# Backward steps of a bidirectional recurrence: queues in program order, z's loads ahead of late stores, and output rows split by VectorE where they are made

## The chip, the core and the metric

The kernel runs on one core of a Trainium2 chip. It uses all engines of that core: TensorE (PE) for matmuls, VectorE (DVE), ScalarE (ACT) and GpSimd (POOL) for the rest, and SyncE (SP), whose queue issues every DMA of the part that matters here. The metric is the device time of one execution in microseconds (us); less is better.

## The reference

The model has two layers over 2048 latent tokens and 256 context tokens of width 1024. The change lies in layer 1, which is cut here to what it computes:

```python
def odd_mixer(h, hc, w_in, conv_w, conv_b, w_a, b_a, w_i, b_i, lam, w_out, need_ctx):
    xr, g = _split(h @ w_in, (C_WIDTH, C_WIDTH))
    z = depthwise_conv(xr, conv_w, conv_b)             # and z_c from the context
    for d, reverse in ((0, False), (1, True)):
        a_c, b_c = rglru_coeffs(z_c, w_a[d], b_a[d], w_i[d], b_i[d], lam[d])
        s_c = linear_scan(a_c, b_c, 0, reverse)
        h0 = s_c[:, 0] if reverse else s_c[:, -1]
        a_l, b_l = rglru_coeffs(z, w_a[d], b_a[d], w_i[d], b_i[d], lam[d])
        s_l = linear_scan(a_l, b_l, h0, reverse)
        h_lat = s_l if h_lat is None else h_lat + s_l
    return (h_lat * silu(g)) @ w_out

def rglru_coeffs(z, w_a, b_a, w_i, b_i, lam):          # z @ w in 4 diagonal blocks of 256
    r, ig = sigmoid(z @ w_a + b_a), sigmoid(z @ w_i + b_i)
    log_a = -LRU_C * r * softplus(-lam)
    return exp(log_a), sqrt(-expm1(2 * log_a)) * (ig * z)

x = x + gate * odd_mixer(...)                          # then a final RMSNorm
```

All of it is fp32.

## The kernel before

The 18 tiles of 128 tokens are worked as 9 pairs of 256 tokens (`L = NPAIR = 9`; pair 0 is the context). An fp32 product is made of three matmuls: each operand is split into a rounded high part and the rest (`split`: a copy on ACT or a CAST on DVE or POOL, then a subtract), and `mm3` multiplies high by high, low by high and high by low. Channels lie on the partitions, 8 tiles of 128, which are worked as four blocks `b` of 256 channels (tiles of 128x512: two channel tiles by 256 tokens).

Layer 1 is one pipeline of steps `s` = 0 to 24, in a loop that writes the program order out by hand. Each step has a projection, a gate part, or both:

- projection: `xr` (the first half of `w_in`, `xr_mm`) of pair `s` in steps 0 to 8; `g` (`g_mm`) in steps 9 to 16; the output (`out_mm`) in steps 17 to 24. Each is four groups of matmuls into PSUM, `px` 0 to 3.
- gates: forward for pair `s - 3` in steps 3 to 11, backward in steps 12 to 20, in the pairs' order 0, 8, 7, 6, 5, 4, 3, 2, 1. A step's gate part is, for each `b`, `gates_mm` (the matmuls `pr` and `pig` with the split tile `zhl`), `gates_act` (two sigmoids on ACT that read `r` and `ig`, and POOL's multiply of `ig` by `z`); then `coeff` and `root` (tanh, exp and square root on ACT, three operations on DVE for each `b`), and `scan` for blocks 0 and 1, and for 2 and 3. In the backward direction the scan's result is added to the forward one (`hf`) and multiplied by the gate projection (`gs`), both read back from DRAM.
- `zsplit` splits `z` of the next step's pair into `zhl`, its block 2 behind the fourth gate matmuls of the step. The order of a step on ACT is: sigmoids of the four blocks, `zhl` of blocks 0 to 3 in between, then the coefficients.

What is carried between steps lies in DRAM: `zs` (z by pair), `hfs` (forward results), `gs_`, `y1s` (the products that the output projection reads), `x1s`. PE, ACT and DVE run in the order of this program from step 1 on (`tc.manual_schedule`); SP's queue and POOL are ordered by the scheduler. The four `wo` tiles (2 MB each, in two halves of 1 MB) are loaded from `kept` copies by `hook`s: `wo`[0] and [1] in step 16, `wo`[2] and [3] in step 17. In step 17 `px` 0 and 1 use the first two, `px` 2 and 3 the last two. For the output `op_load` brings `y1s` back as `opr`, and `op_split` splits it, in steps 17 to 20 by ACT copies and POOL subtracts, later with DVE subtracts.

The `post` of a projection's group 3 is deferred into the next step (`tails`): in the steps with `g` the `gs` of `px` 3 is made and stored behind the sigmoids of block 0 in program order of the next step, and on DVE behind the scans of the step before.

Of the kernel before, what the change touches and what calls it, by code (L numbers as in the profile page):

```python
# [33 lines left out]
U_AT = 5  # L34
T_PE = 14
MOD_AT = 8
WO1_AT = (2, 4, 6, 8, 10, 11, 12, 13)
# [3 lines left out]
def backbone_kernel(ctx: ExitStack, tc: tile.TileContext, a, out):  # L41
# [968 lines left out]
    L = NPAIR  # L1010
    order = [0] + list(range(L - 1, 0, -1))

    with ExitStack() as c4:
# [13 lines left out]
        def halves_load(s):  # L1027

            for q in range(4):
# [16 lines left out]
        def op_split(s, k):  # L1046
            raw = opr.pop((s, k))
            tag = "zhl" if s > 2 * L + 2 and (s - 2 * L - 3) % 2 == 0 else "h1p"
            for q in range(2):
                t = b1.tile([P, 2, 2, U], F32R, tag=tag, name="op", bufs=4)  # L1050
                split(t[:, 0], t[:, 1], raw[:, 2 * q:2 * q + 2], eng_lo=dve if s > 2 * L + 2 else pool)
                for c in range(2):
# [76 lines left out]
        def scan(d, i, bs_):  # L1129
# [3 lines left out]
            for b in bs_:  # L1133
# [7 lines left out]
                e = 0 if d else U - 1  # L1141
                e_c = dve if d and i == order[L - 5] else pool
                e_c.tensor_copy(carry[d][:, 2 * b:2 * b + 2].unsqueeze(2), T[:, :, e:e + 1])  # L1143
            for k in range(2 if i and d else 0):
                for b in bs_:
# [4 lines left out]
                    else:  # L1150
                        dve.scalar_tensor_tensor(T, T, 0.5, hg, ALU.mult, ALU.mult)
            for b in bs_:
                T = ris.pop((d, i, b))[2]
                if i:
                    sp.dma_start((y1s if d else hfs)[i][:, 2 * b:2 * b + 2], T)

# [42 lines left out]
        def g_mm(s, i, b):  # L1199
# [10 lines left out]
            return mm, post  # L1210

        def out_mm(s, i, b):
            x, half = divmod(b, 2) if s > 2 * L - 1 else (b % 2, b // 2)
# [7 lines left out]
            def post():  # L1221
                if half == 0:
                    xts[t] = []
                    for h in range(2):
                        xt = b1.tile([P, 512], F32, tag="gs", name="xt", bufs=4)
                        sp.dma_start(xt, x1s[t][:, 512 * h:512 * h + 512])
                        xts[t].append(xt)
                    xts[t].append(b1.tile([P, 2], F32, tag="ss", name="ss", bufs=2))
                xt, ss, po = xts[t][half], xts[t][2], pxs.pop(b)
                dve.tensor_tensor(xt, xt, po, ALU.add)  # L1230
                act.activation(po, xt, AF.Square, accum_out=ss[:, half:half + 1])  # L1231
                if late:
                    late.pop()()
                end = s == 3 * L - 3 and x == 1
                if half == 0:
# [5 lines left out]
                if end:  # L1241
                    og = b1.tile([P, 512], F32, tag="G", name="og", bufs=1)
                    dve.tensor_tensor(og, xt, FG[:, 512:], ALU.mult)
# [62 lines left out]

        def z_load(s):
            nx = gate(s + 1)
            if nx and nx[0]:
                for b in range(4):  # L1310
                    sp.dma_start(z_tile(*nx, b), zs[nx[1]][:, 2 * b:2 * b + 2])

        def step(s):
# [21 lines left out]

            z_load(s)
            if s + 1 < 2 * L - 1:
                halves_load(s + 1)
            first = early(s) and s != 2 * L - 1
            if first:  # L1340
                op_split(s, 0)
            G(gmm, 0)
            G(gates_act, 0)
            tail(3)
            if early(s) and not first:
                op_split(s, 0)
# [37 lines left out]
            hook("s0")  # L1384
            if source(s + 1) and s + 1 >= 2 * L - 1:
                for k in range(2):
                    op_load(s + 1, k)
                    if not early(s + 1):
                        op_split(s + 1, k)
            if E:  # L1390
                post(0)
            G(scan, (0, 1))
            mm(3)
            if not E:
                post(2)
            elif s > 2 * L + 1:
                post(1)
            G(scan, (2, 3))
            n = gate(s + 1)
            if n and n[0] and n[1]:  # L1400
                for b in range(4):
                    load_hg(n[1], b)
# [4 lines left out]
        def early(s):  # L1407

            return 2 * L - 1 <= s <= 2 * L + 2

        tails = []
# [56 lines left out]
```

## Time and profile before

| | us |
|---|---|
| median of 3 runs (1996.14 to 1998.95) | 1996.38 |
| the profiled execution's own time | 1996.66 |
| its span | 1994.9 |
| PE busy in the span | 1897.1 (95%) |
| DVE busy | 1468.3 (74%) |
| ACT busy | 1095.8 (55%) |
| POOL busy | 599.7 (30%) |

The profiled execution's time is 1.76 us more than its span, and 0.28 us above the median. Times in the trace are us from the span's start; L1207 is line 1207 of the kernel. A step is taken to start at its first gate matmul: step 13 at 1583.50, 14 at 1619.48, 15 at 1654.04, 16 at 1689.46, 17 at 1731.82, 18 at 1765.12, 19 at 1811.68, 20 at 1854.90. The number in brackets at the end of a row of a timeline is the time for which the engine was idle before it, and what ended that. The clock in a stretch is what PE was granted, 1.00 being full speed.

### The profile page before, as it was taken

Reading aid. Unit: us, or ns where it says so; the run is one execution under the profiler, and the core shown is the slowest. Engines: PE = TensorE matmul, PEld = TensorE weight load, DVE = VectorE, ACT = ScalarE, POOL = GpSimd, SP = SyncE. Lnnn points to the kernel's source line nnn. Section 1 sums busy time; section 2 is a strip of 40 time slices with the busy share of each in tenths; the row PEclk is TensorE's granted clock in tenths of the full one; section 3 lists DMA queues with packets and bytes.
Section 4 is the critical chain, followed back from the end, with each engine's and each line's share of the span. In section 5 each row is a group of like instructions: output and inputs, shape, how many; then the busy total and the mean of one; then the engine's idle time right before and its main releaser. Section 6 shows DMA issues by size and latency. Waiting matters only on the chain.

```text
span 1994.9 us, 33922 instructions
## 1 busy us (share of the span) xinstructions
PE 1897.1 (95%) x12223; PEld 1699.0 (85%) x12223; DVE 1468.3 (74%) x3103; ACT 1095.8 (55%) x2221; POOL 599.7 (30%) x793
## 2 busy tenths in 40 slices
PE   7889999999999899989999999999999999878998
PEld 3778888988888688778888899999999999867777
DVE  7788989787755687636777663998986666877863
ACT  6656656666645343414545552767667666656621
POOL 2745656454423211200000000434421121334310
PEclk8999999999999899989999999999999999989999
DMA  9355444361344798365656574233565554965442
GB/s 348 125 183 188 160 156 150 134 212 56 122 156 160 251 331 314 122 242 218 247 191 242 200 263 149 75 135 120 207 231 212 183 193 154 323 209 185 133 165 88
DMA packets 184788, 375.80 MB, mean 188 GB/s; under 512 B 18694, under 2 KB 78858, under 8 KB 176428
## 3 DMA queue, kind: packets, MB, share of 16 engines
q1 hardware_dynamic: 184620, 373.64, 53.5%
q8 instruction: 96, 1.57, 0.3%
q14 instruction: 72, 0.59, 0.1%
HBM read 246.41 MB, written 127.17 MB: 187 GB/s over the span
## 4 chain that ended last, share of the span: by engine, by line
PE 70%; DVE 11%; ACT 6%; DMA 5%; issue 5%; POOL 1%; SPq 1%; POOLq 0%; DVEq 0%; ACTq 0%
PE px L89 6%; PE px L90 6%; PE px L91 6%; PE pu L89 4%; PE pu L90 4%; PE pu L91 4%; PE po L90 3%; PE po L89 3%; PE po L91 3%; PE po L572 3%; PE ptp L560 2%; DVE macc L230 2%; PE pg L89 2%; DMA zf<-zs 2%; PE pg L90 2%
## 5 line engine op out<-in xcount | busy, mean ns | idle before, releaser
L89 PE MATMUL px<-op,w 128*128 128x256 f32 x1088 | 308.1, 283 | 0.0
L90 PE MATMUL px<-op,w 128*128 128x256 f32 x1088 | 307.9, 283 | 0.0
L91 PE MATMUL px<-op,w 128*128 128x256 f32 x1088 | 307.9, 283 | 0.0
L90 PEld LDWEIGHTS px<-op,w 128*128 128x128 f32 x1088 | 208.9, 192 | 0.0
L89 PEld LDWEIGHTS px<-op,w 128*128 128x128 f32 x1088 | 208.9, 192 | 0.0
L91 PEld LDWEIGHTS px<-op,w 128*128 128x128 f32 x1088 | 208.9, 192 | 0.0
L542 POOL TENSOR_SCALAR s<-s,ri 128x640 f32<-128x640 f32 (+2 forms) x144 | 133.5, 939 | 97.9 <-DVE ri L539 93.8
L83 ACT ACTIVATE pT<-ptp 128x512 fp32r<-128x512 f32 (+1 forms) x192 | 99.6, 535 | 92.7 <-PE ptp L560 89.5
L534 ACT ACTIVATE s<-s,mn 128x641 f32<-128x641 f32 (+2 forms) x144 | 113.3, 788 | 64.2 <-DVE mn L516 58.6
L1099 POOL TENSOR_TENSOR ig<-ig,zf 128x512 f32<-128x512 f32 x72 | 109.7, 1532 | 97.7 <-ACT ig L1097 89.8
L86 DVE TENSOR_TENSOR zhl<-zf,zhl 128x512 fp32r<-128x512 f32 x72 | 59.8, 838 | 103.4 <-ACT zhl L83 103.1
L572 PE MATMUL po<-pT,v 128*128 128x256 f32 x656 | 130.1, 296 | 6.1 <-DVE pT L86 4.5
L86 DVE TENSOR_TENSOR pT<-ptp,pT 128x512 fp32r<-128x512 f32 (+1 forms) x192 | 114.3, 604 | 23.6 <-ACT pT L83 22.8
L900 DVE STREAM_TRANSPOSE h1T<-hrow 32x256 f32<-32x256 f32 x224 | 97.7, 436 | 31.1 <-ACT hrow L952 28.1
L89 PE MATMUL px<-w,op 128*128 128x512 f32 x256 | 102.9, 402 | 15.8 <-ACT px L1231 15.8
L162 POOL TENSOR_SCALAR ms<-ss 128x1 f32<-128x1 f32 x36 | 10.0, 278 | 350.2 <-ACT junk L160 343.2
L572 PEld LDWEIGHTS po<-pT,v 128*128 128x128 f32 x656 | 98.6, 189 | 17.3 <-DVE pT L86 9.2
L560 PE MATMUL ptp<-ident,s 128*128 128x128 f32 x656 | 103.6, 273 | 3.4 <-POOL s L542 1.9
L1143 POOL COPY carry<-T 128x2 f32<-128x2 f32 x68 | 35.0, 514 | 232.1 <-DVE T L1140 225.7
L90 PE MATMUL px<-w,op 128*128 128x512 f32 x256 | 102.2, 399 | 0.0
L91 PE MATMUL px<-w,op 128*128 128x512 f32 x256 | 101.9, 398 | 0.0
L89 PE MATMUL pr<-zhl,w 128*128 128x256 f32 x288 | 83.4, 289 | 16.7 <-ACT r L1097 16.7
(277 smaller groups left out, 6186.1 us busy)
## 6 DMA issues: line engine op xcount, KB each, us to landing
hp<-h0s SPq DMA_DIRECT2D x45, 1024.0 KB
op<-h1s SPq DMA_DIRECT2D x64, 512.0 KB
mraw<-in_w_mod SPq DMA_DIRECT2D x48, 512.0 KB
h0s<-hT SPq DMA_DIRECT2D x18, 1024.0 KB
h1s<-h1hl SPq DMA_DIRECT2D x36, 512.0 KB
xt<-in_x SPq DMA_DIRECT2D x32, 512.0 KB
gs<-gs SPq DMA_DIRECT2D x64, 256.0 KB
raw<-in_ab_w_in SPq DMA_DIRECT2D x22, 512.0 KB
```

Source lines behind the costliest of these rows:

```text
L83: act.activation(hi, src, AF.Copy)
L86: (eng_lo or dve).tensor_tensor(lo, src, hi.bitcast(F32), ALU.subtract)
L89: pe.matmul(ps, lhsT=lhs(0), rhs=rhs(0), start=first, stop=False)
L90: pe.matmul(ps, lhsT=lhs(1), rhs=rhs(0), start=False, stop=False)
L91: pe.matmul(ps, lhsT=lhs(0), rhs=rhs(1), start=False, stop=last)
L230: dve.scalar_tensor_tensor(acc[:, m], w[:, kk], c, acc[:, m], ALU.mult, ALU.add)
L534: act.activation(s[:, 0:nk], s[:, 0:nk], AF.Exp, scale=-1.0, bias=st["mn"][:, row, i:i + 1], accum_out=st["sm"][:, i:i + 1])
L542: pool.tensor_scalar(s[:, 1:nk], s[:, 1:nk], ri[:, i:i + 1], 0.0, ALU.mult, ALU.add)
L560: pe.transpose(tp[:, x, h], s_t[h][:, 1 + i * P:1 + (i + 1) * P], ident)
L572: pe.matmul(pos[t, g][:, 2 * P * e:2 * P * (e + 1)], lhsT=vl, rhs=pT[:, hl, x], start=i == 0 and hl == 0, stop=i == n - 1 and hl == 1)
L900: dve.transpose(out[o, :, s], src[s, :, o])
L1099: pool.tensor_tensor(res[1], res[1], zfs.pop((d, i, b)), ALU.mult)
```

## The change

1. From step 12 on (`BACK`) SP's queue and POOL also run in program order.
2. The loads of `z` for the gates of a step (`z_load`) are put elsewhere: blocks 0 and 1 at the end of the step two before it, blocks 2 and 3 behind the sigmoids of block 1 in the step before it. The stores of the scans of blocks 2 and 3 and the loads of `hf` and `gs` for them stand behind that (list `lag`), and behind these the loads of the next step's operands (`halves_load`).
3. The products of the four pairs 8, 7, 6 and 5, which steps 13 to 16 make and steps 17 to 20 project, are split by DVE right after the scan (`store`, tile `yhl`: a CAST and a subtract for each block), stored as `y1h` with twice the bytes, and loaded split. In steps 17 to 20 16 copies on ACT and 16 subtracts on POOL go away.
4. The copies of the carry of blocks 2 and 3 in the backward direction go from POOL to DVE.
5. In the output steps ACT's Square writes into SBUF (`sq`) and not over the PSUM tile, and `x1` (`xt`) is loaded ahead: two tiles in step 17, then one after each final tile. The last tile `og` has another tag.

PE's order is unchanged.

```diff
+    y1h = {i: dram.tile([P, 2, KT, U], F32, name=f"y1h{i}") for i in order[1:5]}
...
         def halves_load(s):
+            if s >= 2 * L - 1:
+                src = y1h[order[s - 2 * L + 2]]
+                for q in range(4):
...
+                    sp.dma_start(t.bitcast(F32), src[:, :, 2 * q:2 * q + 2])
...
-                e_c = dve if d and i == order[L - 5] else pool
+                e_c = dve if d and (b > 1 or i == order[L - 5]) else pool
...
+        def store(s, d, i, b, later=False):
+            T = ris.pop((d, i, b))[2]
+            out_, src = (y1s if d else hfs)[i][:, 2 * b:2 * b + 2], T
+            if d and i in y1h:
...
+                split(t[:, 0], t[:, 1], T, dve)
+                out_, src = y1h[i][:, :, 2 * b:2 * b + 2], t.bitcast(F32)
+            def go():
+                sp.dma_start(out_, src)
+            return go if later else go()
...
                 dve.tensor_tensor(xt, xt, po, ALU.add)
-                act.activation(po, xt, AF.Square, accum_out=ss[:, half:half + 1])
+                sq = b1.tile([P, 512], F32, tag="G", name="sq", bufs=1)
+                act.activation(sq, xt, AF.Square, accum_out=ss[:, half:half + 1])
...
             G(gmm, 0)
             G(gates_act, 0)
             tail(3)
...
             G(gmm, 1)
             G(gates_act, 1)
-            if early(s):
-                op_split(s, 1)
+            z_load(s + 1, 2, 3)
+            while lag:
+                lag.pop(0)()
+            if BACK <= s and s + 1 < 2 * L + 3:
+                halves_load(s + 1)
...
+            if s >= BACK - 1:
+                z_load(s + 2, 0, 1)
             if E:
                 post(0)
             G(scan, (0, 1))
...
+            elif put:
+                lag.extend(store(*put, b, True) for b in (2, 3))
+            if n:
+                lag.extend(lambda b=b: load_hg(n[1], b) for b in ((2, 3) if g[0] else range(4)))
...
-            for s in range(1, 3 * L - 2):
+            for s in range(1, BACK):
+                step(s)
+        with tc.manual_schedule(engines={mybir.EngineType.Activation, mybir.EngineType.PE, mybir.EngineType.DVE,
+                                         mybir.EngineType.SP, mybir.EngineType.Pool}):
+            for s in range(BACK, 3 * L - 2):
                 step(s)
```

Where that puts the instructions is shown at two places; the rows are the line, the operation, and what it writes and reads. The first is SP's queue at the turn from step 16 to step 17. In the kernel before it holds the output weights (`w<-kepto`; the copies 9462 and 9567 are the halves of `wo`[2], 9666 and 9771 those of `wo`[3]), `gs` of `px` 2 and 3 of step 16 (`gs_196<-gs`), loads of `hf` and `gs`, and stores of `y1s`:

```order
L133 DMA w<-kepto_9069 128x2x1024
L133 DMA w<-kepto_9266 128x2x1024
L1208 DMA gs_196<-gs 128x512
L133 DMA w<-kepto_9462 128x2x1024
L133 DMA w<-kepto_9567 128x2x1024
L1161 DMA hf<-hfs_190 128x512
L1161 DMA gs<-gs_199 128x512
L1155 DMA y1s_209<-T 128x512
L1161 DMA hf<-hfs_190 128x512
L1155 DMA y1s_209<-T 128x512
```

In the changed kernel the same queue holds, from the `gs` of `px` 3 of step 16 on, two `z` loads for step 18's gates, the late `y1h` stores, the late loads of `hf` and `gs`, the next operands, and then the weights (the other three halves of `wo`[2] and `wo`[3] stand right behind the last row):

```order
L1232 DMA gs_196<-gs 128x512
L1245 DMA xt<-x1s_166 128x512 x2
L1245 DMA xt<-x1s_167 128x512 x2
L1345 DMA zf<-zs_180 128x512 x2
L1177 DMA y1h_13118<-yhl 256x1x512 x2
L1185 DMA hf<-hfs_190 128x512
L1185 DMA gs<-gs_199 128x512
L1185 DMA hf<-hfs_190 128x512
L1185 DMA gs<-gs_199 128x512
L1038 DMA op<-y1h_13116 128x2x512 x4
L134 DMA w<-kepto_9462 128x2x1024
```

The last two `wo` tiles have gone from beside the `gs` stores of step 16 to behind 17 other transfers.

The second place is DVE's order at the scans of blocks 2 and 3 of step 14, which run at the start of step 15. Before, from `gs` of `px` 2 to `gs` of `px` 3 of step 14:

```order
L1207 SCALAR_TENSOR_TENSOR gs<-gs,px 128x512
L1132 TENSOR_TENSOR r<-r,ig 128x512 x2
L1140 SCALAR_TENSOR_TENSOR T<-T,carry_13156,r 128x256 x4
L1149 TENSOR_TENSOR T<-T,hf 128x512 x2
L1151 SCALAR_TENSOR_TENSOR T<-T,gs 128x512 x2
L1207 SCALAR_TENSOR_TENSOR gs<-gs,px 128x512
L86 TENSOR_TENSOR zhl<-zf,zhl 128x512 x3
```

In the changed kernel, behind `gs` of `px` 2 and two splits of blocks 0 and 1:

```order
L1145 TENSOR_TENSOR r<-r,ig 128x512 x2
L1153 SCALAR_TENSOR_TENSOR T<-T,carry_13160,r 128x256 x2
L1156 COPY carry_13160<-T 128x2
L1153 SCALAR_TENSOR_TENSOR T<-T,carry_13160,r 128x256 x2
L1156 COPY carry_13160<-T 128x2
L1162 TENSOR_TENSOR T<-T,hf 128x512 x2
L1164 SCALAR_TENSOR_TENSOR T<-T,gs 128x512 x2
L86 CAST yhl<-T 128x512
L87 TENSOR_TENSOR yhl<-T,yhl 128x512
L86 CAST yhl<-T 128x512
L87 TENSOR_TENSOR yhl<-T,yhl 128x512
L1231 SCALAR_TENSOR_TENSOR gs<-gs,px 128x512
```

The `gs` of `px` 3 now stands behind two carry copies and two more splits. On SP its store stands right ahead of the `z` loads of blocks 2 and 3 in this step too.

## Rows read from the trace of the kernel before

**Rows 1.** Waits on PE, 1380 to 1995 us: total us, times, longest.

```profile
PE pr L89 <- ACT r L1097: 16.7, 5, 7.2
PE px L89 <- ACT px L1231: 15.8, 6, 4.5
```

**Rows 2.** Stretches: us; busy of PE, PEld, DVE, ACT, POOL; clock, DMA, GB/s.

```profile
1583.50:1619.48 35.98, 34.81 (x291) 34.61 (x289) 23.47 (x38) 26.10 (x52) 6.89 (x8) 1.00 0.36 125
1619.48:1654.04 34.56, 34.56 (x291) 34.56 (x289) 24.30 (x35) 23.23 (x46) 8.23 (x8) 1.00 0.61 206
...
1689.46:1731.82 42.36, 36.60 (x291) 36.40 (x289) 32.90 (x51) 30.96 (x58) 8.58 (x8) 0.92 0.78 260
1731.82:1765.12 33.30, 33.30 (x194) 29.55 (x193) 22.97 (x28) 15.81 (x34) 13.42 (x8) 1.00 1.00 358
1765.12:1811.68 46.56, 36.28 (x193) 31.90 (x192) 39.81 (x56) 33.01 (x72) 17.39 (x18) 0.89 0.44 141
1811.68:1854.90 43.22, 36.76 (x193) 31.60 (x192) 36.99 (x48) 27.16 (x60) 17.87 (x19) 0.92 0.52 165
1854.90:1988.20 133.30, 125.07 (x577) 103.47 (x575) 78.44 (x112) 43.78 (x101) 28.84 (x49) 0.97 0.41 137
```

**Rows 3.** First line of the page.

```profile
span 1994.9 us, 33922 instructions
```

**Rows 4.** Timeline of ACT in steps 14 and 15: start, us, idle before.

```profile
1640.20 0.63 ACT L83 ACTIVATE zhl<-zf 128x512 fp32r<-128x512 f32 x1 [8.11 <-DMA zf<-zs]
...
1659.68 0.84 ACT L1097 ACTIVATE r<-pr,cv 128x256 f32<-128x256 f32 x2
...
1680.77 0.63 ACT L83 ACTIVATE zhl<-zf 128x512 fp32r<-128x512 f32 x1 [11.88 <-DMA zf<-zs]
```

**Rows 5.** Timeline of DVE, the backward scans of step 14.

```profile
1662.66 1.29 DVE L1132 TENSOR_TENSOR r<-r,ig 128x512 f32<-128x512 f32 x2
1663.87 2.67 DVE L1140 TENSOR_TENSOR_SCAN T<-T,carry,r 128x256 f32<-128x256 f32 x4
1666.45 2.51 DVE L1149 TENSOR_TENSOR T<-T,hf 128x512 f32<-128x512 f32 x2
1668.89 3.48 DVE L1151 SCALAR_TENSOR_TENSOR T<-T,gs 128x512 f32<-128x512 f32 x2
1672.29 0.67 DVE L1207 SCALAR_TENSOR_TENSOR gs<-gs,px 128x512 f32<-128x512 f32 x1
```

**Rows 6.** Groups by line and shape: busy, mean ns of one | idle before.

```profile
L86 POOL TENSOR_TENSOR op<-opr,op 128x512 fp32r<-128x512 f32 x16 | 27.7, 1751 | 46.7 <-ACT op L83 46.7
...
L457 DVE CAST qs<-r 128x512 fp32r<-128x512 f32 x16 | 6.7, 419 | 2.0 <-POOL r L411 2.0
```

**Rows 7.** One piece of the chain: start, us.

```profile
1789.56 2.31 DMA hf<-hfs
```

**Rows 8.** Timeline of SP: the last two issues of output weights.

```profile
1741.05 1.18 SPq L133 DMA_DIRECT2D w<-kepto  x2
```

**Rows 9.** Stretches of 5 us inside steps 16 and 17.

```profile
1725.00:1730.00 5.00, 5.00 (x44) 5.00 (x43) 2.15 (x5) 4.96 (x8) 0.00 (x0) 1.00 1.03 415
...
1755.00:1760.00 5.00, 5.00 (x24) 4.14 (x23) 0.00 (x0) 0.00 (x0) 0.00 (x0) 1.00 0.95 241
```

**Rows 10.** Timeline of ACT: the first T of steps 19 and 20.

```profile
1840.98 0.89 ACT L1116 ACTIVATE T<-r,sps 128x256 f32<-128x256 f32 x2
...
1880.34 0.89 ACT L1116 ACTIVATE T<-r,sps 128x256 f32<-128x256 f32 x2
```

**Rows 11.** Timeline of DVE, the backward scans of step 19.

```profile
1855.06 4.71 DVE L1140 TENSOR_TENSOR_SCAN T<-T,carry,r 128x256 f32<-128x256 f32 x4
...
1863.35 3.48 DVE L1132 TENSOR_TENSOR r<-r,ig 128x512 f32<-128x512 f32 x2
1866.75 3.71 DVE L1140 TENSOR_TENSOR_SCAN T<-T,carry,r 128x256 f32<-128x256 f32 x4
```

**Rows 12.** Timeline of POOL in the same stretch as rows 5.

```profile
1667.13 6.39 POOL L1099 TENSOR_TENSOR ig<-ig,zf 128x512 f32<-128x512 f32 x4
```

More of the change, by code (lines that the diff above doesn't have):

```diff
@@ L1027, in halves_load @@
         def halves_load(s):
+            if s >= 2 * L - 1:
+                src = y1h[order[s - 2 * L + 2]]
+                for q in range(4):
+                    if s % 2:
+                        t = raws.tile([P, 2, 2, U], F32R, tag="raw", name="op")
+                    else:
+                        t = b1.tile([P, 2, 2, U], F32R, tag="h1p", name="op", bufs=4)
+                    sp.dma_start(t.bitcast(F32), src[:, :, 2 * q:2 * q + 2])
+                    for c in range(2):
+                        ops[s, 2 * q + c] = t[:, :, c]
+                return
             for q in range(4):
@@ L1210, in g_mm, with x1_load @@
             return mm, post
+        x1_due = []
+        x1_next = [2 * i + x for i in order[1:] for x in range(2)]
+        def x1_load():
+            if x1_next:
+                t = x1_next.pop(0)
+                xts[t] = []
+                for h in range(2):
+                    xt = b1.tile([P, 512], F32, tag="gs", name="xt", bufs=4)
+                    sp.dma_start(xt, x1s[t][:, 512 * h:512 * h + 512])
+                    xts[t].append(xt)
+                xts[t].append(b1.tile([P, 2], F32, tag="ss", name="ss", bufs=2))
         def out_mm(s, i, b):
@@ L1221, in post @@
             def post():
[L1222 to L1228, printed above, removed]
+                while x1_due:
+                    x1_due.pop()()
                 xt, ss, po = xts[t][half], xts[t][2], pxs.pop(b)
                 dve.tensor_tensor(xt, xt, po, ALU.add)
-                act.activation(po, xt, AF.Square, accum_out=ss[:, half:half + 1])
+                sq = b1.tile([P, 512], F32, tag="G", name="sq", bufs=1)
+                act.activation(sq, xt, AF.Square, accum_out=ss[:, half:half + 1])
                 if late:
                     late.pop()()
+                    x1_due.append(x1_load)
                 end = s == 3 * L - 3 and x == 1
@@ L1305, in next_conv, with z_load @@
                 conv(nx[1], b)
-        def z_load(s):
-            nx = gate(s + 1)
+        def z_load(s, *bs_):
+            nx = gate(s)
             if nx and nx[0]:
-                for b in range(4):
+                for b in bs_:
                     sp.dma_start(z_tile(*nx, b), zs[nx[1]][:, 2 * b:2 * b + 2])
@@ L1334, in tail @@
                     tails.pop(0)[1]()
-            z_load(s)
-            if s + 1 < 2 * L - 1:
+            if s == BACK - 1:
+                z_load(s + 1, 0, 1)
+            if s < BACK:
                 halves_load(s + 1)
-            first = early(s) and s != 2 * L - 1
-            if first:
-                op_split(s, 0)
             G(gmm, 0)
@@ L1344, in step @@
             tail(3)
-            if early(s) and not first:
-                op_split(s, 0)
+            if s == 2 * L - 1:
+                x1_load()
+                x1_load()
             next_conv(s, 0)
@@ L1384, in step @@
             hook("s0")
[L1385 removed]
+            if source(s + 1) and s + 1 >= 2 * L + 3:
                 for k in range(2):
                     op_load(s + 1, k)
[L1388 to L1389 removed]
+                    op_split(s + 1, k)
+            if s >= BACK - 1:
+                z_load(s + 2, 0, 1)
             if E:
@@ L1392, in step @@
             G(scan, (0, 1))
+            n = gate(s + 1)
+            n = n if n and n[0] and n[1] else None
+            put = g and g[1] and (s, *g) or None
+            if put and not (g[0] and g[1] in y1h):
+                store(*put, 0)
+                store(*put, 1)
+            if n and g[0]:
+                load_hg(n[1], 0)
+                load_hg(n[1], 1)
             mm(3)
@@ L1397, in step @@
                 post(1)
+            if put and g[0] and g[1] in y1h:
+                store(*put, 0)
+                store(*put, 1)
             G(scan, (2, 3))
[L1399 to L1402, printed above, removed]
+            if put and s < BACK:
+                store(*put, 2)
+                store(*put, 3)
+            elif put:
+                lag.extend(store(*put, b, True) for b in (2, 3))
+            if n:
+                lag.extend(lambda b=b: load_hg(n[1], b) for b in ((2, 3) if g[0] else range(4)))
             if E and s <= 2 * L + 1:
```

15 lines of the change are left out of this document (6 added, 9 removed).

## The prediction, made before the changed kernel ran

> **What bounds the kernel now.** I read the table of waits on TensorE (PE) for the last phase first. The change touches only steps 12 to 24, so only their waits can be won. Two kinds stand there: the gate matmuls `pr` wait for ScalarE (ACT) to have read the previous `r` out of PSUM (16.7 us), and the output projections `px` wait for ACT's Square to free their PSUM bank (15.8 us) [rows 1]. The table of stretches shows what the waits cost in each step [rows 2]. Step 14, with PE busy for all of its 34.56 us, is a step without a wait. Step 17 is one for the steps with an output projection: 33.30 us, at full clock. Against them step 13 loses 1.4 us, step 16 7.8 (PE idle, and a clock of 0.92), step 18 13.3 and step 19 9.9. Steps 20 to 24 take 133.30 us; of these 33.30 and four times 21.8 (33.30 less the gate matmuls, 96 of the 288 in step 14's 34.56 us and so 11.5) would be 120.5. So about 45 us of the 1994.9 us span [rows 3] are losses in reach of the change.
>
> What is behind them shows on ACT. The `zhl` copy of block 2 of the next pair, which `zsplit` issues, waits for the DMA that brings `zf`: in steps 14 and 15 it starts at 1640.20 and 1680.77, after 8.11 and 11.88 us of idling [rows 4]. The two are 40.57 us apart, against 34.56 of PE's own step. It is a loop: that copy at 1640.20 lets the gate coefficients go on, these the DVE scans, and these the `r` read at 1659.68, 19.5 us later, on which PE waits. So a step whose block-2 copy begins later than about 20 us into it makes the next step wait (the next `pr` that needs the bank stands some 5.8 us, half of the 11.5, into the next step, and 34.56 + 5.8 - 20.3 is 20). What the loop needs is `zf` of blocks 2 and 3, and that was issued late.
>
> **z's place in the queue.** The diff loads blocks 0 and 1 a step earlier, and puts blocks 2 and 3 before the late stores. But the listing of SP's queue above shows what stands right before `zf` (2,3) in program order: the `gs` store of `px` 3 of the step before. On DVE that value is made behind the scans of blocks 2 and 3 and, in the listing above, behind their `yhl` splits too. So the loop isn't opened: `zsplit`(2), coefficients, four scans, splits, `gs` of `px` 3, its store's issue, `zf`, `zsplit`(2). Its length: from the copy at 1640.20 to the end of that `gs` at 1672.96 it was 32.76 us [rows 4, 5]. Added are four splits (CAST 0.42 [rows 6] and a subtract, 0.67 by the `gs` row of the same shape [rows 5], so 4 x 1.09 = 4.4 us) and two carry copies that come to DVE (0.35 together, an estimate, between nothing and two whole CASTs of 0.42): 37.5 us. An undisturbed 256 KB landing (2.31 us for `hf` [rows 7]) and some 0.5 of issue (an estimate: half of the 1.18 that two issues take [rows 8]) close it at 40.3 us, as good as the 40.57 of before. So I cost the reordering of z at nothing for steps 14 to 16, and step 16 keeps its 7.8; only step 13's 1.4 us go, since its blocks are loaded before the loop has formed (bounds: they stay, or step 16's go too). `zsplit`(2) then starts 1.4 earlier in step 14, at 1638.8, and at 1679.1 in step 15 and 1719.4 in step 16; step 17 begins at 1731.82 - 1.4 = 1730.4.
>
> **What the queue in order does to the weights.** Before, the scheduler issued the last output weights, 1 MB each, by 1741.05 [rows 8]. Now, in the listing of SP above, the four halves of `wo`[2] and `wo`[3] stand behind the `gs` store of `px` 3 of step 16. That value is done at 1719.4 + 37.5 = 1756.9. Behind it and ahead of the weights stand four `xt`, two `zf`, two `y1h`, four `hf`/`gs` and four `op`: with the store 11 pieces of 256 KB and 6 of 512 KB, 6.0 MB. At the rate of the weight loads of before, 415 GB/s [rows 9], this takes 14.5 us; I take 15.5, one more for the mixture of loads and stores. The weights' 4.2 MB take 10.1. With 0.45 of issue and some 2 us until the first lands, the last weight is there at 1785.0. PE wants it for `px` 2 of step 17, at 1730.4 + 11.5 + 2 x 5.45 and a gate wait of 3.5 (1719.4 + 20.3, less 1730.4 + 5.8) = 1756.3. So a wait of some 28 us appears in step 17, which waited for nothing before. Behind it stands a last quarter of `px` 2 (1.4), `px` 3 (5.45) and some 2 us of slow clock, as the stretches with waits show clocks of 0.89 to 0.92 [rows 2]: step 18 starts at 1793.9 rather than 1765.12. Step 17 costs 63.5 us rather than 33.30: **+30.2**. Bounds: the weights wait for nothing else and land by 1756 (0), or at 241 GB/s (below).
>
> **What steps 18 to 24 give back.** While PE waits, DVE, ACT and POOL finish their work, so step 18 starts with nothing behind. Steps 18 and 19 then take 33.30 us: **-13.3** and **-9.9**. Whether they keep it is the loop's matter, seen in ACT's first `T` of each step: 1840.98 and 1880.34, 39.36 us apart [rows 10], more than PE's 33.30. What DVE does in it is slowed by the POOL subtracts of `op_split`, 1.75 us each [rows 6], which vanish from steps 17 to 20: two sets of four scans take 4.71 and 3.71 [rows 11] rather than the 2.67 of one with POOL idle [rows 5], and the 3.48 of the pair of multiplies ahead of the second is 2.2 above the 1.29 of an undisturbed pair [rows 5]; half of that, 1.1, I put down to `op` and half to an `ig`, which stays. These 4.2 us less 0.35 of carry copies make the loop 35.5 us. The sixteen POOL subtracts (27.7 us [rows 6]) and the sixteen ACT copies leave engines that are busy for 13 to 33 us of steps that long or longer [rows 2], so beyond this they count nothing. The `y1h` tiles double what is stored and loaded for four pairs, 4.2 MB more each way over eight steps; the DMA engines' share in them is 0.36 to 0.78 but for step 17's 1.00 [rows 2], so I count them there alone, in the 6.0 MB. POOL in program order has each `ig` behind two carry copies, which come before ACT's sigmoids anyway: nothing, and one copy's length if it were not so. After the long wait `T` of step 18 comes about 15.3 us behind PE's start (11.5 of gate matmuls and some 4 of sigmoids, an estimate), so that of step 20 comes 15.3 + 2 x 2.2 = 19.7 behind its start, where before it came 1880.34 - 1854.90 = 25.44 behind: **-5.7**. The Square writes to SBUF, so DVE's addition frees the bank and not ACT, the 0.6 us of an ACT copy of that shape earlier [rows 4]; I count it once, **-0.6**, since the late engine is DVE, at which these waits end (bounds 0 and the 15.8 us of that wait [rows 1], of which much is already in steps 18 and 19). Loading `x1` ahead is hidden (SP's loads were ahead of DVE there), and so is the output's other tile.
>
> **The sum:** -1.4 + 30.2 - 13.3 - 9.9 - 5.7 - 0.6 = -0.7 us on the profiled execution's 1996.66 us (span 1994.9 and 1.76 around it), which lies 0.28 above the median of 1996.38. So 1995.7 us by the median: two large things that cancel.
>
> **Does the split meet POOL?** In the loop's 32.76 us the two additions of `hf` took 2.51 and the two multiplies by `gs` 3.48, twice and nearly three times the 1.29 of an undisturbed pair, while POOL did its four `ig` multiplies, 6.39 us for the four [rows 5, 12]: 3.4 us of the loop are such meetings. I keep them at 3.4, though the splits are new work that could meet POOL as well. The Trainium skill's "SBUF — State Buffer", section "Who interferes with whom", says that VectorE and GpSimd hold a shared port pair for a whole instruction and that the other fully blocks, for operations with two SBUF inputs and for casts in a two-port mode. The rows agree for the former; of a CAST against POOL no row here tells. By that rule each of the four `ig` would always meet something, which is the second rival's sum below; by the rows alone the sum above stands.
>
> **The rivals.**
> 1. Faster: the `ig` multiplies come when DVE is at a scan or idle, and meet nothing. For it: POOL is now free of `op` and each `ig` can start once ACT is done. Against it: in the loop of step 14 all four met DVE [rows 5, 12], and in that of step 19 one did. The loop is then 3.4 us shorter, `gs` of `px` 3 of step 16 comes 3 x 3.4 = 10.2 us earlier, the weights too: 1985.5. If also z were at PE's pace (`zsplit`(2) 20 us into each step), it would be 1981, the lowest that the weights' place allows.
> 2. Slower, by the meetings: all four `ig` block DVE for their full length, 4 x 1.3 with nothing in their own way, 5.2 us instead of 3.4: 1.8 more in three passes, 5.4: 2001.1. It is what the rule of the Trainium skill's "SBUF — State Buffer" would make of it.
> 3. Slower, by the stream: in step 17 of before, with `hf`, `gs`, `xt` and stores mixed, the DMA engines were at a share of 0.95 and moved only 241 GB/s [rows 9]. At that rate the 6.0 MB take 25.0 us rather than 15.5: 2005.2. It decides below about 300 GB/s (20.2 us), where the time passes the bound of what can be told.
> 4. The weights' place costs nothing, because the queue's DMAs run beside one another or `gs` comes much earlier. Then step 17 keeps 33.30 and some 3.5, step 18 loses about as much as before, and the -5.7, -0.6 and some of step 19's 9.9 are left: about 1987.
>
> **How the numbers follow.** Forecast 0.48 (its own range 1990 to 2001), rival 1 0.20, rival 2 0.08, rival 3 0.12, rival 4 0.07, and 0.05 for what I don't see. A difference of 0.2% is 4.0 us, about what a measurement of this kernel can tell from no change: the bounds are 1992.4 and 2000.4. Faster: rivals 1 and 4, and a fifth of the forecast, 0.37. Slower: rivals 2 and 3 with a few hundredths of the forecast, 0.24. The same: 0.39. The range reaches from rival 1 with some of its further end, 1982, to rival 3, 2005.
>
> **What would show it.** Right, if the trace of after has PE idle 20 to 35 us in step 17, waiting for a DMA into `w`; if steps 18 and 19 take 33 to 34 us each; if no POOL `op` is left before step 21; and if ACT's `zhl` copies of block 2 still wait for `zf` in steps 14 to 16 with some 40 us between them. Wrong, if step 17 has no such wait (then faster), or if steps 18 and 19 still lose 10 us (then slower by as much): the first would mean that I misread when the queue's head comes free, the second that the loop and not POOL's subtracts sets these steps.

## The result, and the profile after

The changed kernel takes 2029.73 us (median of 5 runs, 2027.55 to 2032.35) against 1996.38 us: 1.0162 times the time of before, with a 95% interval of 1.0147 to 1.0177. It is slower by 33 us, and the forecast of 1995.7, with its range up to 2005, was wrong.

The profiled execution took 2032.35 us, with a span of 2030.6. These are its stretches by step, in the columns of rows 2: steps 14 to 17, 18, 19 and 20 to 24.

```profile
1621.84:1656.40 34.56, 34.56 (x291) 34.56 (x289) 25.28 (x39) 22.74 (x46) 6.67 (x4) 1.00 0.62 215
1656.40:1691.08 34.68, 34.68 (x291) 34.62 (x289) 26.48 (x40) 15.96 (x35) 6.58 (x6) 1.00 0.58 172
1691.08:1735.47 44.39, 36.31 (x290) 36.11 (x289) 33.53 (x53) 25.39 (x52) 6.57 (x6) 0.92 0.65 203
1735.47:1803.58 68.11, 38.40 (x195) 32.92 (x193) 49.64 (x83) 30.93 (x60) 7.11 (x6) 0.77 0.87 317
1803.58:1836.88 33.30, 33.30 (x194) 29.54 (x192) 18.23 (x29) 22.51 (x50) 7.91 (x10) 1.00 0.56 189
1836.88:1877.66 40.78, 35.58 (x194) 30.94 (x192) 24.02 (x38) 21.02 (x45) 8.76 (x12) 0.92 0.55 181
1877.66:2024.00 146.34, 129.43 (x577) 106.69 (x575) 77.99 (x124) 46.41 (x106) 18.93 (x41) 0.94 0.41 140
```

The last stretch is drawn 0.3 us past the end of the last matmul at 2023.66, so steps 20 to 24 are taken as 146.0 us below.

Against [rows 2] step 16 costs 2.0 us more, step 17 34.8 more, step 18 13.3 less, step 19 2.4 less, and steps 20 to 24 12.7 more; step 13 loses its 1.4 and step 15 0.7. Nearly all of the rest of the span's 35.7 us lies ahead of step 8, which starts 3.8 us later (at 1414.48 rather than 1410.70), in a part that runs in the same order on every engine in both traces; from there to step 13 each step takes 34.56 us in both. In the thirteen profiled executions of this study step 12 starts anywhere from 1547.97 to 1553.56 us, so these 3.8 us say nothing of the change.

The forecast by step, its terms and what was measured:

| step | before | forecast | after | after less forecast |
|---|---|---|---|---|
| 16 | 42.36 | 42.36 | 44.39 | +2.0 |
| 17 | 33.30 | 63.5 | 68.11 | +4.6 |
| 18 | 46.56 | 33.3 | 33.30 | 0.0 |
| 19 | 43.22 | 33.3 | 40.78 | +7.5 |
| 20 to 24 | 133.30 | 127.0 | 146.0 | +19.0 |

Step 18 went as forecast, and step 17 nearly so, with the wait for the output weights as the largest event. What was missed lies for the most part behind them, in steps 19 to 24: 26.5 us. The waits of PE from 1384 us on (total, times, longest):

```profile
PE px L90 <- DMA w<-kepto: 22.9, 2, 22.1
PE px L90 <- DVE xt L1262: 19.6, 6, 5.2
PE pr L90 <- ACT r L1110: 17.1, 3, 8.1
```

The first is new; `pr` waits as in [rows 1], 17.1 us for 16.7. The second is the wait that was on ACT's Square (15.8 us): the bank is now freed by DVE's addition, and it waits longer. Why shows in what DVE itself waits for. In step 19 it stands still once for a load of `x1`, and PE's one wait of that step, 5.2 us, is for the addition behind it:

```profile
1863.91 0.69 DVE L1262 TENSOR_TENSOR xt<-xt,px 128x512 f32<-128x512 f32 x1 [11.77 <-DMA xt<-x1s]
```

DVE's waits from 1875 us on are these:

```profile
DVE op L87 <- ACT op L84: 30.6, 4, 11.0
DVE xt L1262 <- DMA xt<-x1s: 19.0, 4, 7.5
DVE xt L1262 <- PE px L92: 13.6, 4, 4.8
```

In the kernel before, the same table over its steps 20 to 24 has the addition waiting for PE itself most of the time, that is, for its proper input:

```profile
DVE xt L1230 <- PE px L91: 36.4, 10, 4.8
DVE xt L1230 <- DMA xt<-x1s: 6.7, 2, 3.5
DVE op L86 <- ACT op L83: 5.4, 4, 1.5
```

So DVE is late now because two loads are late: `opr`, which ACT splits and DVE subtracts from, and `x1`. SP's timeline at one such turn shows the order that makes them late, and SP's own waits from 1590 us on (second fence) that an `x1` load stands there until an out store has landed:

```profile
1931.90 0.92 SPq L1245 DMA_DIRECT2D xt<-x1s  x2
1938.09 0.92 SPq L1177 DMA_DIRECT2D y1s<-T  x2
1939.90 1.13 SPq L1291 DMA_DIRECT2D out<-xt  x2
1944.14 0.89 SPq L1245 DMA_DIRECT2D xt<-x1s  x2
1945.11 0.86 SPq L1056 DMA_DIRECT2D opr<-y1s  x2
```

```profile
SPq L1245 <- DMA out<-xt: 20.4, 22, 3.5
```

`opr` needs nothing that is late: its rows were stored several steps ago. But it stands behind the last scan's store, behind an out store, and behind an `x1` load that waits until that out store has landed and its tile is free. ACT's copy starts at 1951.51, 6.4 us behind that issue, and DVE's subtract, which stands ahead of the addition in DVE's order, idles 11.05 us for it. (For this copy the profile names nothing that released it; the next two start 6.65 and 6.43 us behind their issue and are put down to the load of `opr`.)

```profile
1952.17 2.51 DVE L87 TENSOR_TENSOR op<-opr,op 128x512 fp32r<-128x512 f32 x4 [11.05 <-ACT op L84]
1954.61 0.68 DVE L1262 TENSOR_TENSOR xt<-xt,px 128x512 f32<-128x512 f32 x1
```

In the chain that ended last (followed back from the last instruction, at each step to what released it) the two `x1` loads of steps 19 and 20 are pieces of their own, 7.66 and 5.76 us, where the undisturbed load of [rows 7] took 2.31:

```profile
1781.57 15.02 DMA w<-kepto
1856.23 7.66 DMA xt<-x1s
...
1900.06 5.76 DMA xt<-x1s
```

What the prediction said of the loop and of the weights can be read off too. ACT's `zhl` copies of block 2, in steps 14, 15, 16 and 17:

```profile
1641.82 0.63 ACT L84 ACTIVATE zhl<-zf 128x512 fp32r<-128x512 f32 x1 [7.37 <-DMA zf<-zs]
...
1684.72 0.63 ACT L84 ACTIVATE zhl<-zf 128x512 fp32r<-128x512 f32 x1 [10.28 <-DMA zf<-zs]
...
1727.84 0.63 ACT L84 ACTIVATE zhl<-zf 128x512 fp32r<-128x512 f32 x1 [10.50 <-DMA zf<-zs]
...
1774.19 0.63 ACT L84 ACTIVATE zhl<-zf 128x512 fp32r<-128x512 f32 x1 [13.69 <-DMA zf<-zs]
```

The first two are 42.90 us apart and the next two 43.12: the loop is not opened, it is a little longer than the 40.57 of [rows 4]. And SP's queue in step 17 goes in just the order of the listing, from `gs` of `px` 3 on:

```profile
1765.90 0.33 SPq L1232 DMA_DIRECT2D gs<-gs  x1
1766.28 2.62 SPq L1245 DMA_DIRECT2D xt<-x1s  x4
1768.95 0.90 SPq L1345 DMA_DIRECT2D zf<-zs  x2
...
1775.37 3.62 SPq L1038 DMA_DIRECT2D op<-y1h  x4
1779.04 3.15 SPq L134 DMA_DIRECT2D w<-kepto  x4
```

### The profile page after: what moved, and what is told of

Its sections match the earlier page's. It is cut to its first block, busy times and chain, and to the rows that moved or that the text cites. A ratio compares the mean times of both kernels' runs of the same rounds, so it can differ in the third digit from the quotient of the medians.

```text
span 2030.6 us, 33925 instructions
## 1 busy us (share of the span) xinstructions
PE 1905.4 (94%) x12223; PEld 1705.3 (84%) x12223; DVE 1469.1 (72%) x3151; ACT 1089.9 (54%) x2205; POOL 556.1 (27%) x761
## 4 chain that ended last, share of the span: by engine, by line
PE 70%; DVE 12%; DMA 7%; ACT 5%; issue 4%; SPq 1%; POOL 0%; DVEq 0%; POOLq 0%; ACTq 0%
PE px L90 7%; PE px L91 7%; PE px L92 7%; PE pu L90 3%; PE pu L92 3%; PE pu L91 3%; PE po L91 3%; PE po L90 3%; PE po L92 3%; PE po L573 3%; PE ptp L561 2%; DVE macc L231 2%; PE pg L90 2%; PE pg L92 2%; PE pg L91 2%
## 5 line engine op out<-in xcount | busy, mean ns | idle before, releaser
L90 PE MATMUL px<-w,op 128*128 128x512 f32 x256 | 105.0, 410 | 42.5 <-DMA w<-kepto 22.9
L901 DVE STREAM_TRANSPOSE h1T<-hrow 32x256 f32<-32x256 f32 x224 | 97.7, 436 | 31.1 <-ACT hrow L953 28.1
L1110 ACT ACTIVATE r<-pr,cv 128x256 f32<-128x256 f32 x144 | 60.5, 473 | 85.2 <-PE pr L92 66.6
L91 PE MATMUL px<-w,op 128*128 128x512 f32 x256 | 103.3, 404 | 0.0
L92 PE MATMUL px<-w,op 128*128 128x512 f32 x256 | 103.2, 403 | 0.0
L90 PE MATMUL pr<-zhl,w 128*128 128x256 f32 x288 | 83.5, 290 | 17.1 <-ACT r L1110 17.1
```

Of the source, the lines that this page charges most:

```text
L90: pe.matmul(ps, lhsT=lhs(0), rhs=rhs(0), start=first, stop=False)
L91: pe.matmul(ps, lhsT=lhs(1), rhs=rhs(0), start=False, stop=False)
L92: pe.matmul(ps, lhsT=lhs(0), rhs=rhs(1), start=False, stop=last)
L901: dve.transpose(out[o, :, s], src[s, :, o])
L1110: act.activation(r[:, j], gps[b][nm][:, j], AF.Sigmoid, bias=bias[:, c:c + 1])
```

## The experiments

Three theories stood after this. The first: the places of a few transfers in SP's program order are the whole loss, namely the weights, `gs` of `px` 3 ahead of `z`, `opr` and `x1`. The second: program order as such is too stiff for these queues, wherever things stand in it. The third: the split costs, through DVE's longer loop and the doubled bytes. Each run is shown with its ratio to the kernel before, timed on the same chip.

**Weights ahead.** The changed kernel, with one place moved:

```diff
+        hooks[2 * L - 2, "m3"] = hooks.pop((2 * L - 1, "z3")) + hooks.pop((2 * L - 1, "c0"))
...
+            mm(3)
+            hook("m3")
             if n and g[0]:
                 load_hg(n[1], 0)
                 load_hg(n[1], 1)
-            mm(3)
```

> The changed kernel, with the loads of wo[2] and wo[3] moved in SP's program order from behind the next operands in step 17 to behind px 3 of step 16; nothing else. Theory: TensorE's 22 us wait for w in step 17 of the changed kernel is the place of these four loads in the queue. Then it goes wholly. But the pause had let the other engines catch up, so step 18 loses about 10 us again: 2029.7 - 22 - 8 (the half-speed clock and pr wait of step 17, in part) + 10, about 2008 to 2014. Rival: the stream is at its limit and the loads are late wherever they stand: no less than 2025.

Measured 2023.04 us, ratio 1.0124 (1.0109 to 1.0139). The wait for `w` is gone wholly, so it was the place in the queue. But the time falls by 7 us, not 16 to 22. Between 1730 and 1830 us PE waits for `r` 17.6 us, in three waits, and step 17 takes 42.35 us, step 18 45.86 and step 19 44.53, where the changed kernel had 68.11, 33.30 and 40.78: the 26 us won in step 17 are given back but for some 9 in the next two.

```profile
PE pr L90 <- ACT r L1110: 17.6, 3, 10.2
```

The pause had been hiding the loop's loss. The expected size was wrong: step 17 was to gain some 30 us and gained 26, and the loop was to take back 10 and took 16.

**opr ahead.** The changed kernel, with the load of the output operands moved:

```diff
+            if source(s + 1) and s + 1 >= 2 * L + 3:
+                for k in range(2):
+                    op_load(s + 1, k)
             G(gates_act, 0)
...
                 for k in range(2):
-                    op_load(s + 1, k)
                     op_split(s + 1, k)
```

> The changed kernel, with the loads opr of the output operands for steps 21 to 24 moved in SP's program order to the top of the step before, ahead of the x1 loads and out stores; nothing else. Theory: in steps 20 to 24 the changed kernel is 12 us slower than the kernel before because opr stands behind x1 loads, which wait for the landing of an out store; ACT's split then waits for opr and DVE's subtract, queued ahead of the addition that frees a PSUM bank, waits for ACT. Then these 12 us go, and a few more: 2014 to 2018. Rival: it is x1 itself that comes late there (DVE's wait for xt, 30.7 us in all): not under 2025.

Measured 2025.13 us, ratio 1.0127 (1.0107 to 1.0147). DVE's wait for ACT's `op` falls from 30.6 to 9.0 us, and from the start of step 20 to the start of the last matmul it takes 138.36 us where the changed kernel took 145.61: 7.3 of the 12.7 us. The time missed the 2014 to 2018 that were expected. The wait for `x1` stays, so the rival holds the other half:

```profile
DVE xt L1262 <- PE px L92: 25.9, 8, 4.8
DVE xt L1262 <- DMA xt<-x1s: 20.2, 6, 7.9
DVE op L87 <- ACT op L84: 9.0, 6, 2.9
```

**The scheduler's queues.**

```diff
-        with tc.manual_schedule(engines={mybir.EngineType.Activation, mybir.EngineType.PE, mybir.EngineType.DVE,
-                                         mybir.EngineType.SP, mybir.EngineType.Pool}):
+        with tc.manual_schedule(engines={mybir.EngineType.Activation, mybir.EngineType.PE, mybir.EngineType.DVE}):
             for s in range(BACK, 3 * L - 2):
```

> The changed kernel, with SP's queue and POOL ordered by the scheduler again from step 12 on; the split rows y1h, the carry copies on DVE, the Square into SBUF and x1's loads ahead stay. Theory: program order on SP's queue is what costs, by the weights in step 17 and by opr and x1 in steps 19 to 24; without it all of these go and the gains of the rest are left: 1975 to 1992. Rival: the new work of the split (DVE's 16 casts and subtracts, twice the bytes) costs as well: 2000 or more.

Measured 1987.54 us, ratio 0.9949 (0.9933 to 0.9965). With nothing changed but the order of SP and POOL, 42 us go, and the rest of the change is worth 0.5%. The third theory is out as a cause of the loss. Steps 17 to 19 take 37.89, 41.95 and 38.20 us, and from step 20 to the start of the last matmul it is 130.54. This run puts SP and POOL back together; that POOL's program order is not the loss shows in the runs with three and four moves below, which keep it.

**z ahead of gs.** The changed kernel, with the store of `gs` of `px` 3 behind `z`, and in step 17 also the loads of the first two `x1` tiles:

```diff
-                sp.dma_start(gs_[i][:, 2 * b:2 * b + 2], pair(gs))
+                def put():
+                    sp.dma_start(gs_[i][:, 2 * b:2 * b + 2], pair(gs))
+                if b == 3 and s >= BACK - 1:
+                    lag.append(put)
+                else:
+                    put()
...
-            if s == 2 * L - 1:
-                x1_load()
-                x1_load()
...
             while lag:
                 lag.pop(0)()
+            if s == 2 * L - 1:
+                x1_load()
+                x1_load()
```

> The changed kernel, with the store of gs of px 3 put behind the loads of z for blocks 2 and 3 in SP's order (and the two x1 tiles of step 17 behind it); nothing else. Theory: z of blocks 2 and 3 waits in the queue behind that store, which closes the loop from zsplit to zsplit at 43 us. With z ahead, zsplit of block 2 no longer waits in steps 14 to 16, steps 15 to 17 keep 34.6 us each before px, and the weights' turn comes some 10 to 20 us earlier: 2029.7 - 9 (step 16) - 4 (step 17) - 10 to 18: 2000 to 2010. Rival: z waits as long for the release of its slot by POOL's ig, or for the transfer itself: no change, 2025 to 2032.

Measured 2008.5 us, ratio 1.0051 (1.0036 to 1.0066). Steps 13 to 16 take 34.56 us each, without a wait, and step 17 54.83. From 1590 to 1780 us ACT waits for `zf` only twice, 5.7 us in all, both times in step 17. In the stretches of steps 16 and 17:

```profile
1691.80:1726.36 34.56, 34.56 (x291) 34.56 (x290) 31.62 (x52) 25.00 (x48) 6.47 (x4) 1.00 0.76 264
1726.36:1781.19 54.83, 36.02 (x194) 30.77 (x193) 40.05 (x64) 22.21 (x46) 7.12 (x6) 0.81 0.89 332
```

One store of 256 KB in the wrong place cost some 21 us: it closed the loop, and the loop set when the weights' turn came. Step 16, in which the store alone was moved, falls by 9.8 us. In step 17, which falls by 13.3, the four `x1` loads moved too, but the same transfers stand ahead of the weights in both orders. The weights' own place still costs: PE idles 18.0 us ahead of `px` 2 of step 17. The profile puts that wait down to DVE's addition of `hf`, which these matmuls don't read; they start 10.6 us behind the issue of the weights, for 10.2 in the changed kernel, so it is most likely the weights again.

**The moves together**, on the changed kernel, with SP and POOL in program order. Three moves are the three above. Four add `x1`, whose loads the changed kernel keeps back (`x1_due`) until the next addition:

```diff
             def post():
-                while x1_due:
-                    x1_due.pop()()
...
                 if late:
                     late.pop()()
-                    x1_due.append(x1_load)
+                    x1_load()
```

> The changed kernel with the three moves together: weights behind px 3 of step 16, gs of px 3 behind z, opr at the top of the step before; SP and POOL stay in program order. Theory: the loss of the changed kernel is these places in SP's order and nothing that belongs to program order as such or to the split: steps 13 to 16 at 34.6 us, step 17 some 35, step 18 36 to 42, step 19 some 41 (x1 still behind op), steps 20 on some 138: a time of 1983 to 1992, under the kernel before. Rival: with the pauses gone the DVE loop (four splits longer) becomes the limit of steps 17 to 19 and takes back what the pauses hid: 1996 or more.

Measured 1988.24 us, ratio 0.9959 (0.9944 to 0.9974): within the expectation. Step 17 takes 33.31 us, step 18 39.23, step 19 45.21, and from step 20 to the start of the last matmul 138.12.

> The kernel with three moves, and x1's two loads issued right behind the out stores that free their tiles, not at the next addition. Theory: in steps 19 to 21 of the changed kernel TensorE's bank waits for DVE's addition, which waits for x1, issued behind op, y1s, hf and gs (two pieces of 6 to 8 us on the chain). These waits then go: 6 to 12 us under the kernel with three moves, 1972 to 1984. Rival: SP now stands at the landing of an out store (2 to 3.5 us each time) with z and opr behind it: no gain, or 1 to 5 us more.

Measured 1976.5 us, ratio 0.9895 (0.9881 to 0.991), 12 us under three moves, the upper end of what was expected. Step 19 falls to 36.63 us and the rest to 132.15. So the second theory is out as well: with four transfers moved, program order is faster than the scheduler's.

**The Square alone.** First the kernel before with the Square's result in SBUF (and `og` in T's tiles), then the changed kernel with the scheduler's queues and the Square over PSUM.

```diff
-                act.activation(po, xt, AF.Square, accum_out=ss[:, half:half + 1])
+                sq = b1.tile([P, 512], F32, tag="G", name="sq", bufs=1)
+                act.activation(sq, xt, AF.Square, accum_out=ss[:, half:half + 1])
...
-                    og = b1.tile([P, 512], F32, tag="G", name="og", bufs=1)
+                    og = b1.tile([P, 512], F32, tag="T", name="og", bufs=4)
```

> The kernel before, with the Square's result in SBUF (and og in T's tiles); nothing else of the change. Theory: the px bank is free 0.6 to 0.8 us earlier at each of the some six waits of 15.8 us in all, which are mostly DVE's lateness: 0.5 to 4 us faster, 1993 to 1997. Rival: this edit is what makes the changed kernel's other parts pay (10 us with the scheduler's queues): 1990 or less.

Measured 1994.09 us, ratio 0.9994 (0.9981 to 1.0007): no change that can be told.

> The changed kernel with the scheduler's queues (SP, POOL), and the Square over PSUM as before. Theory: what made that kernel some 10 us faster than the one before is the vanished POOL subtracts and ACT copies of steps 17 to 20, not the Square: 1988 to 1992. Rival: the Square carries it: 1995 or more.

Measured 1990.27 us, ratio 0.9964 (0.9949 to 0.9978), against 0.9949 (0.9933 to 0.9965) with the Square in SBUF. The two ratios are 3 us apart and their intervals overlap; by their ends up to 9 us (0.9978 less 0.9933) would be allowed. The traces are closer: from the start of step 13 to the end of the last matmul the two take 395.8 us with the Square in SBUF and 396.6 over PSUM.

**The split alone, and z further ahead.** The first is the kernel with four moves without `y1h`: its diff takes the four pairs through `y1s`, `opr` and `op_split` again.

```diff
-    y1h = {i: dram.tile([P, 2, KT, U], F32, name=f"y1h{i}") for i in order[1:5]}
+    y1h = {i: dram.tile([P, 2, KT, U], F32, name=f"y1h{i}") for i in order[:0]}
...
-                split(t[:, 0], t[:, 1], raw[:, 2 * q:2 * q + 2])
+                split(t[:, 0], t[:, 1], raw[:, 2 * q:2 * q + 2], eng_lo=dve if s > 2 * L + 2 else pool)
...
```

> The kernel with four moves, without the split rows: pairs 8, 7, 6, 5 go through y1s and opr, and steps 17 to 20 split them by 16 ACT copies and 16 POOL subtracts again; DVE's 16 casts and subtracts of steps 13 to 16 are gone. Theory: in steps 13 to 16 TensorE is the bound and DVE's splits cost nothing, in steps 17 to 20 POOL's subtracts slow DVE's scans by some 4 us a step: 6 to 14 us slower than the kernel with four moves, 1982 to 1991. Rival: once the queue is in a good order the loop has slack, and the split's doubled bytes cost as much as it brings: 1974 to 1979.

Measured 1984.83 us, ratio 0.9934 (0.991 to 0.9957), 10.6 us above the kernel with four moves as timed beside it (the last run below). Steps 18 and 19 of this kernel, and then of the kernel with four moves:

```profile
1757.03:1803.16 46.13, 38.09 (x194) 32.95 (x192) 39.78 (x57) 31.82 (x68) 16.37 (x16) 0.89 0.45 150
1803.16:1844.05 40.89, 36.47 (x193) 31.54 (x192) 34.54 (x46) 24.97 (x55) 15.85 (x16) 0.92 0.49 161
```

```profile
1757.34:1797.76 40.42, 35.78 (x194) 31.78 (x193) 34.08 (x55) 28.51 (x62) 9.53 (x12) 0.92 0.78 251
1797.76:1834.25 36.49, 33.85 (x194) 29.51 (x192) 30.14 (x45) 22.43 (x50) 9.10 (x12) 1.00 0.66 224
```

The split rows bring 5.7 and 4.4 us there (DVE is busy 5.7 and 4.4 us less, POOL 6.8 less in each; a pair of scans that meets a POOL subtract takes 2.42 us, the same pair without it 1.38), and steps 13 to 17 are the same 34.56 and 33.31 in both.

```diff
             if put and g[0] and g[1] in y1h:
-                store(*put, 0)
-                store(*put, 1)
+                lag.extend([store(*put, b, True) for b in (0, 1)])
```

> The kernel with four moves, and the stores y1h of blocks 0 and 1 put behind z of blocks 2 and 3 too. Theory: in step 17 of the kernel with four moves ACT's copy of block 2 still waits 13 us for zf, since z stands behind those stores, which wait for DVE's splits; step 18 loses 6.8 us to it. With z ahead step 18 takes 33.3 to 36: 3 to 7 us under the kernel with four moves, 1969 to 1974. Rival: the weights' 4 MB ahead of z in the queue and not the stores make z late: no more than 1 us.

Measured 1971.31 us, ratio 0.9869 (0.9844 to 0.9893). Its four timed runs, 1969.76 to 1972.32, lie below the four of the kernel with four moves timed beside it, 1973.53 to 1975.49. Step 18 takes 37.41 us rather than 40.42, and not the 33.3 to 36 that were expected. But ACT's copy of block 2 in step 17 still idles 10.41 us for `zf` (12.94 with four moves), so the stores were the smaller part of that wait; whether the rest is the weights' 4 MB ahead in the queue was not tried. This is the fastest version that was run, 1.3% under the kernel before.

> The kernel with four moves once more, to compare the other two with on the same chip: 1974 to 1979 as before.

Measured 1974.19 us, ratio 0.9885 (0.986 to 0.9909), by which the two above are judged.

## Why the prediction was wrong

**z's place in the queue: right, the size a little off, and near the old one by luck.** The loop stayed closed by `gs` of `px` 3, as the order listing said, and opening it in the fourth experiment took 21 us off. From the copy at 1684.72 to the end of that `gs` at 1722.72 it is 38.0 us, for the 37.5 worked out. What was short is the landing: the `zf` load behind it, issued at 1723.17, is a piece of 4.65 us on the chain, where an undisturbed load of 2.31 and 0.5 of issue were put in. That makes the period 43.0 and not 40.3, 2.7 us in each of two passes: `gs` of `px` 3 of step 16 was stored 4.8 us later than worked out (1765.90 less the 3.8 of the late start is 1762.1; the forecast has 1756.9 and 0.45 of issue), step 16 cost 2.0 more, and most of step 17's 4.6 is that. The trace of the kernel before could have told the landing. On its chain the `zf` loads that ended the waits of the two copies in [rows 4] are these:

```profile
1634.43 5.75 DMA zf<-zs
1673.54 7.21 DMA zf<-zs
```

So the 40.57 us between those copies held a landing of 7.21, and the forecast's 40.3 one of 2.31 behind a longer way through DVE. That the two numbers were "as good as" the same was a coincidence.

**The weights: right.** PE waited 22.1 us in one piece for `w`, where some 28 had been put in; part of the difference is the gate wait ahead of it, 6.8 us rather than 3.5. Step 17 cost 34.8 us where 30.2 had been put in. From the `gs` store's issue to the last weight, at 1781.57 + 15.02 = 1796.59, it is 30.7 us for a reckoned 28. In the stretches of that time the last column is the rate:

```profile
1770.00:1775.00 5.00, 0.00 (x0) 0.00 (x0) 0.15 (x1) 0.81 (x2) 0.00 (x0) 0.50 0.97 321
1775.00:1780.00 5.00, 0.00 (x0) 0.00 (x0) 1.77 (x3) 4.97 (x11) 0.00 (x0) 0.50 1.02 328
1780.00:1785.00 5.00, 0.00 (x0) 0.00 (x0) 5.00 (x11) 4.97 (x11) 0.00 (x0) 0.50 1.01 351
1785.00:1790.00 5.00, 0.75 (x2) 0.69 (x3) 5.00 (x9) 3.33 (x7) 0.49 (x1) 0.50 1.04 421
```

It was 321 to 351 GB/s in the first three, between the 241 of the third rival and the 415 of [rows 9], and 421 in the last. The first experiment showed the wait to be the place in the queue and nothing else.

**What steps 18 to 24 give back: wrong, and this step is the failure.** Its first part held: after the pause step 18 took 33.30 us. Its mechanism held too: without the split, steps 18 and 19 take 5.7 and 4.4 us more, with DVE busy for as much longer beside POOL's subtracts, near the 4.2 a step that were read from [rows 11]. What failed is the sentence "Loading `x1` ahead is hidden (SP's loads were ahead of DVE there)". That was read from a queue which the scheduler had ordered, and the change takes the scheduler away. The weights were looked up in the new order; `x1` and `opr` behind step 18 were not, and `opr` isn't named in that part at all. There they stand behind stores that wait for scans, and behind one another: step 19 took 40.78 us and not 33.3, and steps 20 to 24 146.0 and not 127.0. ACT's first `T` of steps 18, 19 and 20, on which the -5.7 was built, shows the moment:

```profile
1821.44 0.89 ACT L1129 ACTIVATE T<-r,sps 128x256 f32<-128x256 f32 x2
...
1868.01 0.89 ACT L1129 ACTIVATE T<-r,sps 128x256 f32<-128x256 f32 x2
...
1908.66 0.89 ACT L1129 ACTIVATE T<-r,sps 128x256 f32<-128x256 f32 x2
```

In step 18 it comes 17.9 us behind the step's start, where 15.3 had been put in; in step 19 it is 31.1, since ACT's Square, ahead of it in ACT's order, waits for the addition that idles 11.77 us for `x1`; and in step 20 it is 31.0 rather than 19.7, later than the 25.4 of before. The second experiment (`opr` ahead: 7.3 us off the last part) and the step from three moves to four (`x1`: step 19 from 45.21 to 36.63, the last part from 138.12 to 132.15) show both. Together these 7.3 and 6.0 us are about the 12.7 that steps 20 to 24 lost against before. Whether the -5.7 would come behind a long wait with both loads in time was not tried: where both are in time the wait is gone too, and the first `T` of step 20 comes 25.5 us behind its start with four moves, as before.

**The Square: right in being small.** The 0.6 us could not be told from nothing by the times; the two traces with the scheduler's queues, one execution each, lie 0.8 apart.

**The rivals.** None was the case. The slower ones looked for the loss in steps 14 to 17, with 5.4 and 9.5 us, and the one on POOL's meetings rests on a point that the trace of after bears out without the price it gave. Of the sixteen `yhl` CASTs there the four that start while POOL multiplies take 0.90 to 1.52 us, the other twelve 0.41 or 0.42. One of each, with the multiply that the first one meets:

```profile
1707.83 1.29 POOL L1112 TENSOR_TENSOR ig<-ig,zf 128x512 f32<-128x512 f32 x1 [0.64 <-POOL ig L1112]
...
1708.27 1.14 DVE L86 CAST yhl<-T 128x512 fp32r<-128x512 f32 x1
...
1710.04 0.42 DVE L86 CAST yhl<-T 128x512 fp32r<-128x512 f32 x1
```

These rows agree with what the Trainium skill's "SBUF — State Buffer" (section "Who interferes with whom") says of casts that take the port pair shared with GpSimd. The price here, 0.7 us for the CAST shown, is inside the 38.0 us of the loop, which came out 0.5 above the forecast.

## What to carry to other kernels

When a queue goes from the scheduler's order to program order, every transfer that it issues has a new place, and each has to be looked up against what stands ahead of it and waits: not only the one that the change is about. A load that needs nothing late must not stand behind a store that waits for the end of a chain; here four such places made 53 us, the difference between the changed kernel and the one with four moves. And a long pause hides the losses behind it, so that taking it away alone gives back only part: in the first experiment 7 of 26 us.

## What was not expected of the hardware

A 256 KB load behind other traffic took 4.65 to 8.49 us to land on the chain (`zf` and `x1` above; 8.49 in the second experiment) against 2.31 undisturbed, at DMA shares of 0.41 to 0.65 over the steps of the changed kernel. In the 7.66 us of the `x1` load of step 19, behind four loads of 512 KB, the share was 0.98. So a step's mean share says little of a single load's latency. And PE's granted clock fell with the wait: over step 17 it was 0.77, in the stretches from 1770 to 1785 us, without a matmul, 0.50 (1.2 GHz of 2.4), and in step 18, with PE busy throughout, 1.00 again.
